# Moving the overflow branch of a mixture-of-experts layer ahead of its first gate product

## The chip, the cores and the metric

The kernel runs on one core of one Trainium2 chip. The metric is device time in microseconds (us) of one execution. A core has five engines with a queue of instructions each: PE (matrix products; its weight loads, PEld, are shown apart), DVE and ACT (vectors), POOL, and SP, which here only issues transfers (DMA) from the chip's memory. The engines wait for each other through semaphores.

## What is computed

Two layers, each a token mixer (a convolution module in the first, retention in the second) and then a mixture of experts over 256 tokens of width 1024. Each token goes to its best group of 8 experts and there to the best two. Cut to what matters:

```python
combine = jnp.sum(jax.nn.one_hot(expert_id, N_EXPERTS) * gates[..., None], axis=1)
for e in range(N_EXPERTS):                        # 32 experts, width 512
    h = jax.nn.silu(xt @ w_gate[e]) * (xt @ w_up[e])
    y = y + combine[:, e:e + 1] * (h @ w_down[e])
x = layer_norm(alpha * x + y)
```

All in float32. The weights of the experts are 6 MiB each, 192 MiB a layer, and are read once.

## The kernel before, in words

**Capacity and overflow.** Only an expert's own tokens go through its weights. The kernel gives each expert 64 places (`CAP`). `posm` holds for each token and expert the place it has, or 0; a token with place 65 or higher overflows. What overflows is worked off by `overflow`, a loop over all experts that is entered by a branch alone: `over` marks the overflowing places, a small product sums it over the tokens (`flag` in the trace, L1028), DVE adds the 64 sums up (L1031) and makes an integer of it (L1032). All five engines load that number into a register (L1203) and branch on it (L1208). With these inputs no token overflows, so every engine jumps over the body. On PE and SP the body is long (84 rows on PE as merged below, nearly 150 on SP).

**The experts.** `experts` goes through the 32 experts; each has four steps `gate_up(e, i)` of 8 matmul instructions of 512 columns (gate and up, two slices of the width each), then `hidden` (SiLU on ACT, a product on DVE, which gives `h`), `turn` (transposes of `h` on PE, `hT`), and later, two experts at a time, `down` and `scatter`. The tokens of four experts at a time are collected by one-hot products: `gather(qd, qs)`, in four quarters of the width. A quarter (`gp` in the trace) is 8 matmul instructions of 256 columns and a copy from the accumulators by ACT; the quarters 0 and 1 fill `xghi`, which the steps 0 and 1 of an expert read, the quarters 2 and 3 fill `xglo` for the steps 2 and 3.

**The weights' homes.** `Weights` loads pieces of 1 MiB in the order of use into a ring of 12 homes (`RING`), and beside it into a few others. `used(n)` gives the homes of consumed pieces back, and at once issues the next loads on SP's queue, each of which waits there until PE has read the home's old piece. So the loads run ahead of PE by the ring's size at most. When an expert stage starts, all homes are full.

**The order around the change.** It is written out by hand. In `experts`, before: two quarters of the first gather, then the rest of the routing on DVE (`rest`, which gives the gates and the marks), `gate_up(0, 0)`, the other two quarters, `turned` (transposes of `posm`, and the flag's product), `gate_up(0, 1)` to `(0, 3)`, and then `extra`, which loads the flag and branches. Its scratch (`spare`) takes two homes of the ring, so the two homes that step (0, 3) gives back are counted free only behind it (`W.used(2)`). Behind the branch come the scaling of `cur` by ACT (L1228), `hidden(0)` and the next expert. The two homes that step (0, 1) gave back are loaded ahead of the branch. Where the body is jumped over, each engine runs a short replacement that brings the semaphores to where the body would have left them; SP's part of it waits for all transfers in flight on its eight semaphores (L1208).

Of the kernel before, what the change touches and what calls it, by code (L numbers as in the profile page):

```python
# [10 lines left out]
F32 = mybir.dt.float32  # L11
# [4 lines left out]
OP = mybir.AluOpType  # L16
AX = mybir.AxisListType

P = 128
# [6 lines left out]
CAP = 64  # L26
# [5 lines left out]
RING = 12  # L32
# [17 lines left out]
class Weights:  # L50
# [4 lines left out]
    def __init__(self, nc, ringp, splitp, handp, pieces, layers):  # L55
        self.nc, self.ringp, self.splitp, self.handp = nc, ringp, splitp, handp
        self.pieces, self.layers = pieces, layers
        self.next = 0
        self.tiles, self.parts = {}, {}
        self.order = [2 * i + j for i, (_, sp) in enumerate(pieces) if sp for j in range(2)]  # L60
        self.nsplit = 0
        self.nused = 0
        self.at = 0
        self.between = []
        self.stop = len(pieces)
        self.room = {"ring": RING, "own": 0, "split": 0, "once": 0}
        self.taken = []
        self.own = None

    def home(self, i):  # L70
        for a, b in self.layers:
# [19 lines left out]
    def load(self, n=99):  # L91

        for _ in range(n):
            while self.next in self.tiles:
                self.next += 1
            for i in range(self.next, len(self.pieces)):
                home, kind = self.home(i)
                if i not in self.tiles and (self.room[home] or home != "once"):
                    break
            else:  # L100
                return
            if not self.room[home]:
                return
            self.room[home] -= 1
            src = self.pieces[i][0]
            dma = self.nc.sync.dma_start
            if home == "split" or kind:
                m = src.shape[1] // 2
                v = []
                for h, tag in enumerate(("hd", "hd") if kind == "hand" else ("hi", "lo")):  # L110
                    t = (self.handp if kind == "hand" else self.splitp).tile([P, m, 1024 // m], F32, tag=tag, name=f"w{i}{h}")
                    dma(t, src[:, h * m:(h + 1) * m])
                    v += [t[:, k] for k in range(m)]
                self.tiles[i] = v
                continue
            t = (self.own if home == "own" else self.ringp).tile([P, 2048], F32, tag=home, name=f"w{i}",
                                                                 bufs=2 if home == "own" else RING)
            if isinstance(src, list):
                v = t.rearrange("p (g a b) -> p g a b", g=2, b=P)
                for g in range(2):  # L120
                    dma(v[:, g], src[g])
                    if self.between:
                        self.between.pop(0)()
                v = [v[:, g] for g in range(2)]
            else:
                v = t.rearrange("p (a b) -> p a b", a=src.shape[1])
                dma(v, src)
                if not self.pieces[i][1]:
                    v = [v[:, k] for k in range(src.shape[1])]
            self.tiles[i] = v  # L130
# [32 lines left out]
        t, self.tiles[i] = self.tiles[i], None  # L163
        return t

    def spare(self, name):

        t = self.ringp.tile([P, 2048], F32, tag="ring", name=name, bufs=RING)
        return t[:, 0:1024], t[:, 1024:2048]

    def used(self, n=1):

# [14 lines left out]
def trunk(ctx, tc, a, out):  # L187
    nc = tc.nc
    ET = mybir.EngineType
    V, S, G, PE = nc.vector, nc.scalar, nc.gpsimd, nc.tensor  # L190
# [8 lines left out]
    def acc1(name):  # L199
        return psum.tile([P, 512], F32, tag="acc", name=name, bufs=4)  # L200
# [5 lines left out]
    def sm1(name, dt=F32):  # L206
        return psum.tile([P, 512], dt, tag="sm", name=name, bufs=4)
# [14 lines left out]
    for p in range(NE // 2 - 1):  # L222
        e, both = 2 * p + 2, (2 * p, 2 * p + 1)
# [37 lines left out]
    W = Weights(nc, ringp, splitp, handp, pieces, layers)  # L261
# [31 lines left out]
    onesb = consts.tile([P, P], BF, name="onesb")  # L293
# [134 lines left out]
    mark = {}  # L428
# [519 lines left out]
    def route(L, ep, lg, comb, posm, posT, flag):  # L948
# [3 lines left out]
        def words(n):  # L952
            used[0] += n
            return space[:, used[0] - n:used[0]]

        def t2(n):
            t = words(2 * n)
            return t.rearrange("p (a b) -> p a b", a=2) if n > 1 else t

        def t2b():  # L960

            return words(NE).bitcast(BF).rearrange("p (a b) -> p a b", a=2)

        def bc(x, n):
            return x[:, :, None].to_broadcast([P, 2, n])
# [40 lines left out]

        def rest():

            pg = t2(1)
            V.tensor_reduce(pg, gs, op=OP.add, axis=AX.X)  # L1010
            g1 = t2(1)
            V.scalar_tensor_tensor(g1, ex, 1.0, pg, op0=OP.add, op1=OP.mult)
            V.reciprocal(g1, g1)
            V.tensor_tensor(ex, ex, g1, op=OP.mult)
            V.tensor_tensor(oh1, oh1, bc(g1, 32), op=OP.mult)
            V.tensor_tensor(oh2, oh2, bc(ex, 32), op=OP.mult)
            V.tensor_tensor(comb, oh1, oh2, op=OP.add)
            posb = t2b()
            V.tensor_copy(posb, posm)
            over = t2b()  # L1020
            V.tensor_scalar(over, posm, CAP + 1.0, None, op0=OP.is_ge)

            def turned():
                pt = sm1("posT", BF)
                for tt in range(2):
                    PE.transpose(pt[:NE, tt * P:(tt + 1) * P], posb[:, tt], identb)
                fp = sm1("flag")
                PE.matmul(fp[:1, 0:64], onesb[:, 0:1], over.rearrange("p a b -> p (a b)"), start=True, stop=True)  # L1028
                V.tensor_copy(posT, pt[:NE, :T])
                ff = words(1)[:1]  # L1030
                V.tensor_reduce(ff, fp[:1, 0:64], op=OP.add, axis=AX.X)  # L1031
                V.tensor_copy(flag, ff)  # L1032

            return turned

        mark["rest"] = rest

    def experts(L, mp, ep, x1h, x1l, comb, posm, posT, flag):
# [22 lines left out]
        def gate_up(e, i):  # L1061

            if i == 0:
                gus[e] = acc1(f"gu{e}")
            if i % 2 == 0:
                gws[e] = W.take(), W.take()
            for k in range(2):
                kt = i * 2 + k
                l = xg[e // 4][kt // 4][:, kt % 4, e % 4 * CAP:(e % 4 + 1) * CAP]
                for m, w in enumerate(gws[e]):  # L1070
                    PE.matmul(gus[e][m * CAP:(m + 1) * CAP], l, w[i % 2 * 2 + k], start=kt == 0, stop=kt == KT - 1)  # L1071
            if i % 2:
                gws.pop(e)
                if (e, i) != (0, 3):
                    W.used(2)

        def hidden(e):
            gu = gus.pop(e)
# [122 lines left out]
        def extra():  # L1201

            rv = nc.values_load(flag[0:1, 0:1], min_val=0, max_val=T * NE)  # L1203
            (wts, big), mid = [W.spare(f"ov{n}{L}") for n in range(2)]
            mid = [ep.tile([P, 512], F32, tag="gl", name="ovgl")[:CAP], *[m[:CAP] for m in mid]]
            row = ep.tile([P, T], F32, tag="s0", name="ovs", bufs=2)
            pair = [acc1(f"ov{n}") for n in range(2)]
            with tc.If(rv > 0):  # L1208
                overflow(L, x1h, x1l, comb, posm, wts, big, mid, row, pair)
        fin, seeds = {}, {}  # L1210
        identr = ep.tile([P, P], F32R, name="identr")
        G.tensor_copy(identr, ident)
        W.stop = layers[L][1]
        one_hots(0)
        warm(WARM[5])
        gather(0, range(2))
        turned = mark["rest"]()
        for e in range(NE):
            for i in range(4):
                gate_up(e, i)  # L1220
                if e == 0 and i == 0:
                    gather(0, range(2, 4))
                    turned()
                if e == 0 and i == 3:
                    extra()
                    W.used(2)
                    for tt in range(2):
                        S.activation(cur[:, tt], cur[:, tt], AF.Copy, scale=ALPHA)  # L1228
                if i == 3:
                    hidden(e)  # L1230
                run(e, i)
                if e + 4 < NE and e % 4 == 1 and i == 0:
                    one_hots(e // 4 + 1)
                if e + 2 < NE and e % 4 == 2:
                    gather(e // 4 + 1, [i])
                if (e, i) in ROWS_AT:
                    n = ROWS_AT.index((e, i))
                    if n == 0:
                        rows = mp.tile([P, 2048], F32, tag="x1h", name=f"rows{L}")
                    spread_rows(L, rows, n)  # L1240
            if L == 0 and e == 3:
                mark["rot"] = rotary_tables()
            if L == 0 and e == 10:
                mark["rot"]()
# [139 lines left out]
```

## Time and profile before

| | |
|---|---|
| median of 3 runs | 1292.09 us (1291.44 to 1296.46) |
| profiled execution | 1292.11 us |
| its span in the trace | 1290.4 us |
| PE busy | 1246.8 us (97%) |
| DVE, ACT, POOL busy | 490.5, 338.7, 139.9 us |
| data moved | 459.45 MB, mean 356 GB/s |

PE's busy time counts matmuls that wait in the array's queue for their operands, so 97% does not mean that PE works at its peak. The transfers run at 425 to 427 GB/s in the middle of both expert stages. The stages of the experts last from about 138 to 597 us and from about 820 us to the end; the places that the change touches are the first 20 us of each.

### The profile page before, as it was taken

The numbers are of one execution on the slowest core, as the hardware profiler recorded it, in microseconds if no ns is written. First come the engines' busy times: TensorE is split into PE (matmuls) and PEld (weight loads), VectorE is DVE, ScalarE is ACT, GpSimd is POOL, SyncE is SP. The second block draws the span as 40 slices with busy tenths as digits, with TensorE's granted clock in tenths as the row PEclk, the third lists the DMA queues.
The fourth block names the chain that finished last, engine by engine and source line by source line (L and its number), as shares of the span: only waits on it lengthen the run. The fifth ranks groups of instructions, "written<-read, shape, count | busy, mean of one in ns | idle before, by whom it ended". The sixth has DMA issues, their size and how long they took to land.

```text
span 1290.4 us, 15546 instructions
## 1 busy us (share of the span) xinstructions
PE 1246.8 (97%) x6163; PEld 659.6 (51%) x6163; DVE 490.5 (38%) x863; ACT 338.7 (26%) x561; POOL 139.9 (11%) x167
## 2 busy tenths in 40 slices
PE   9989899999999999998999999899999999999996
PEld 7867444343443334434997788544443444444432
DVE  5986313222232222235566755413222232222224
ACT  4655311121111111123434543411111211111111
POOL 4882008100000000002130000000000000000000
PEclk9999799999999999998999999899999999999998
DMA  9935699999999999999865556699999999999993
GB/s 321 398 116 175 224 391 426 425 425 425 424 427 425 425 425 425 426 427 409 290 197 180 179 196 197 261 382 405 422 425 426 425 427 425 425 426 424 427 426 137
DMA packets 102390, 459.45 MB, mean 356 GB/s; under 512 B 8258, under 2 KB 25442, under 8 KB 59554
## 3 DMA queue, kind: packets, MB, share of 16 engines
q1 hardware_dynamic: 102082, 457.92, 88.2%
q8 instruction: 53, 0.87, 0.3%
q0 software_dynamic: 80, 0.26, 0.1%
q10 hardware_dynamic: 144, 0.15, 0.1%
q14 instruction: 31, 0.25, 0.0%
HBM read 457.25 MB, written 1.05 MB: 355 GB/s over the span
## 4 chain that ended last, share of the span: by engine, by line
PE 60%; DMA 25%; DVE 2%; ACT 1%; issue 0%; DVEq 0%; SPq 0%; ACTq 0%
PE gu L1071 22%; DMA w<-in_moe_w_up_dram 11%; DMA w<-in_moe_w_down_dram 11%; PE y L1126 10%; PE gp L1057 4%; PE sc L1158 3%; DMA w<-in_moe_w_gate_dram 2%; PE vg L788 2%; PE vg L790 2%; PE vg L789 2%; PE hT L1091 1%; PE qk L771 1%; PE qk L770 1%; PE qk L768 1%; PE wo L656 1%; PE wo L657 1%
## 5 line engine op out<-in xcount | busy, mean ns | idle before, releaser
L1071 PE MATMUL gu<-w,xghi 128*64 128x512 f32 x1024 | 250.5, 606 | 1.9 <-DMA w<-in_moe_w_up_dram 1.0
L1126 PE MATMUL y<-w,h 128*64 128x512 f32 x960 | 240.9, 596 | 7.5 <-DMA w<-in_moe_w_down_dram 7.4
L1071 PE MATMUL gu<-w,xglo 128*64 128x512 f32 x1024 | 242.6, 600 | 0.0
L1082 DVE TENSOR_TENSOR h<-gl,gu 64x512 f32<-64x512 f32 x64 | 67.7, 1058 | 368.4 <-ACT gl L1080 368.4
L1126 PEld LDWEIGHTS y<-w,h 128*64 128x64 f32 x960 | 73.4, 137 | 151.8 <-issue 134.2
L1071 PEld LDWEIGHTS gu<-w,xglo 128*64 128x64 f32 x1024 | 69.7, 137 | 117.5 <-issue 107.9
L1071 PEld LDWEIGHTS gu<-w,xghi 128*64 128x64 f32 x1024 | 67.8, 137 | 110.4 <-issue 101.2
L143 DVE TENSOR_TENSOR l<-w,h 128x1024 fp32r<-128x1024 f32 x66 | 83.6, 1269 | 68.7 <-ACT h L142 67.1
L142 ACT ACTIVATE h<-w 128x1024 fp32r<-128x1024 f32 x72 | 75.7, 1058 | 88.0 <-PE vg L790 31.7
L1080 ACT ACTIVATE gl<-gu 64x512 f32<-64x512 f32 x64 | 37.7, 589 | 229.0 <-PE gu L1071 229.0
L1104 ACT ACTIVATE h<-hT 128x256 f32<-128x256 f32 x64 | 24.7, 385 | 261.3 <-PE hT L1101 148.9
L1162 DVE TENSOR_TENSOR cur<-sc,cur 128x512 f32<-128x512 f32 x112 | 69.5, 683 | 19.0 <-PE sc L1158 19.0
L1113 DVE COPY gsl<-hT 64x1 f32<-64x1 f32 x60 | 9.4, 156 | 169.8 <-ACT h L1104 169.4
L1057 PE MATMUL gp<-oh,x1h 128*128 128x256 f32 x256 | 59.0, 313 | 3.7 <-DVE route L1010 3.7
L1057 PEld LDWEIGHTS gp<-oh,x1h 128*128 128x128 f32 x256 | 40.5, 196 | 40.5 <-issue 39.6
L1146 ACT ACTIVATE yh<-y,gsl 128x512 fp32r<-128x512 f32 x60 | 41.2, 687 | 75.8 <-PE y L1126 75.6
L466 PE MATMUL pw<-xT,w 128*128 128x256 f32 x256 | 57.8, 381 | 1.6 <-DMA w<-in_conv_w_pw_dram 1.6
L499 POOL TENSOR_TENSOR gp<-gp,gt 128x256 f32<-128x256 f32 x76 | 56.3, 742 | 22.0 <-ACT gt L498 16.6
L143 POOL TENSOR_TENSOR l<-w,h 128x1024 fp32r<-128x1024 f32 x6 | 14.9, 2516 | 364.1 <-ACT h L142 364.1
L466 PEld LDWEIGHTS pw<-xT,w 128*128 128x128 f32 x256 | 48.2, 190 | 8.9 <-issue 2.5
L1057 PE MATMUL gp<-oh,x1l 128*128 128x256 f32 x256 | 52.6, 288 | 0.0
L1139 DVE TENSOR_SCALAR s<-sp,cc 128x256 fp32r<-128x256 f32 x30 | 14.5, 484 | 86.0 <-PE sp L1136 86.0
(322 smaller groups left out, 1585.1 us busy)
## 6 DMA issues: line engine op xcount, KB each, us to landing
w<-in_moe_w_up_dram SPq DMA_DIRECT2D x116, 1024.0 KB, 15.8
w<-in_moe_w_down_dram SPq DMA_DIRECT2D x112, 1024.0 KB, 17.1
w<-in_moe_w_gate_dram SPq DMA_DIRECT2D x106, 1024.0 KB, 14.7
w<-in_ret_w_qkvg_dram SPq DMA_DIRECT2D x24, 1024.0 KB, 13.2
w<-in_moe_w_gate_dram SPq DMA_DIRECT2D x44, 512.0 KB, 14.7
w<-in_moe_w_down_dram SPq DMA_DIRECT2D x32, 512.0 KB, 17.2
w<-in_moe_w_up_dram SPq DMA_DIRECT2D x24, 512.0 KB, 17.2
w<-in_conv_w_pw_dram SPq DMA_DIRECT2D x16, 512.0 KB, 6.3
```

The costliest lines, as they stand in the source:

```text
L142: self.nc.scalar.activation(hi, w, AF.Copy)
L143: (self.nc.gpsimd if pool else self.nc.vector).tensor_tensor(lo, w, hi.bitcast(F32), op=OP.subtract)
L466: PE.matmul(ps[:, 1 - g], w[g][:, kt], xT[:, kt], start=kt == 0, stop=kt == KT - 1)
L499: G.tensor_tensor(gps[c], gps[c], t, op=OP.add)
L1057: PE.matmul(ps[:, k], src[:, tt, q * 2 + k], o[:, tt].rearrange("p e c -> p (e c)"), start=i == 0, stop=i == 3)
L1071: PE.matmul(gus[e][m * CAP:(m + 1) * CAP], l, w[i % 2 * 2 + k], start=kt == 0, stop=kt == KT - 1)
L1080: S.activation(gl, gu[:CAP], AF.Silu)
L1082: V.tensor_tensor(hs[e].rearrange("s k p -> s p k"), gl.rearrange("s (p k) -> s p k", k=4), gu[CAP:].rearrange("s (p k) -> s p k", k=4), o ...
L1126: PE.matmul(ys[pr][b][j * CAP:(j + 1) * CAP], hs[e][:, kt], wds[e][kt % 2][:, n * 512:(n + 1) * 512], start=kt == 0, stop=kt == 3)
L1146: S.activation(yh[:, n], ys[pr][n], AF.Copy, scale=g)
L1158: PE.matmul(ps, s0[pr][ks, tt * P:(tt + 1) * P], ys[pr][i][ks, n if pr >= 0 else 0], start=not held and i == 0, stop=i == 1 and (pr == -1 ...
L1162: V.tensor_tensor(o, ps, o, op=OP.add)
```

## The change

Per expert stage: the marks `over` are computed first in `rest`. `rest` is called ahead of the first gather, and gives back two functions: `flagged` (the flag's product and its two steps on DVE) and `turned` (the transposes of `posm`). Then come quarter 0, `flagged`, the quarters 1 and 2, and the branch; behind it `gate_up(0, 0)` and `(0, 1)`, quarter 3, `turned`, and `gate_up(0, 2)`, `(0, 3)`. The scratch of the body no longer takes free homes: `lend` hands out the three last loaded pieces of the ring, the body writes over them, and loads them anew from memory at its end, inside the branch.

```diff
+                if home == "ring":
+                    self.raw[i] = t, v, src
...
-    def spare(self, name):
-
-        t = self.ringp.tile([P, 2048], F32, tag="ring", name=name, bufs=RING)
-        return t[:, 0:1024], t[:, 1024:2048]
+    def lend(self, n):
+
+        held = sorted(i for i, v in self.tiles.items() if v is not None and i in self.raw)[-n:]
+        return [self.raw[i] for i in held]
...
         def rest():
 
+            over = t2b()
+            V.tensor_scalar(over, posm, CAP + 1.0, None, op0=OP.is_ge)
...
-            over = t2b()
-            V.tensor_scalar(over, posm, CAP + 1.0, None, op0=OP.is_ge)
+
+            def flagged():
+                fp = sm1("flag")
+                PE.matmul(fp[:1, 0:64], onesb[:, 0:1], over.rearrange("p a b -> p (a b)"), start=True, stop=True)
+                ff = words(1)[:1]
+                V.tensor_reduce(ff, fp[:1, 0:64], op=OP.add, axis=AX.X)
+                V.tensor_copy(flag, ff)
...
-                if (e, i) != (0, 3):
-                    W.used(2)
+                W.used(2)
...
-            (wts, big), mid = [W.spare(f"ov{n}{L}") for n in range(2)]
-            mid = [ep.tile([P, 512], F32, tag="gl", name="ovgl")[:CAP], *[m[:CAP] for m in mid]]
+            lent = W.lend(3)
+            (wts, big), mid, (sg, _) = [(t[:, 0:1024], t[:, 1024:2048]) for t, _, _ in lent]
+            mid = [sg[:CAP, 0:512], *[m[:CAP] for m in mid]]
...
                 overflow(L, x1h, x1l, comb, posm, wts, big, mid, row, pair)
+                for _, v, src in lent:
+                    nc.sync.dma_start(v, src)
...
-        gather(0, range(2))
-        turned = mark["rest"]()
+        flagged, turned = mark["rest"]()
+        gather(0, [0])
+        flagged()
+        gather(0, [1, 2])
+        extra()
         for e in range(NE):
             for i in range(4):
                 gate_up(e, i)
-                if e == 0 and i == 0:
-                    gather(0, range(2, 4))
+                if e == 0 and i == 1:
+                    gather(0, [3])
                     turned()
                 if e == 0 and i == 3:
-                    extra()
-                    W.used(2)
                     for tt in range(2):
                         S.activation(cur[:, tt], cur[:, tt], AF.Copy, scale=ALPHA)
```

PE's queue at the start of the first expert stage, before (`gp00` to `gp03` are the quarters of the gather, `gu0` is expert 0, `flag` the flag's product, `w` the weights):

```order
L1057 MATMUL gp01_1288<-oh0_1274,x1l_1109 128x256 x2
L1071 MATMUL gu0_1307<-w12_205,xghi0_1276 64x512
...
L1057 MATMUL gp02_1312<-oh0_1274,x1h_1108 128x256 x2
...
L1057 MATMUL gp03_1322<-oh0_1274,x1l_1109 128x256 x2
...
L1028 MATMUL flag_1335<-route0_1225,onesb_126 1x64
...
L1071 MATMUL gu0_1307<-w15_400,xglo0_1277 64x512
L1203 TENSOR_LOAD flag_1113
L1208 COMPARE_AND_BRANCH
...
L1071 MATMUL gu1_1740<-w16_493,xghi0_1276 64x512
```

The same place of PE's queue now:

```order
L1062 MATMUL gp00_1287<-oh0_1274,x1l_1109 128x256 x2
L1028 LDWEIGHTS onesb_126
L1028 MATMUL flag_1297<-route0_1225,onesb_126 1x64
L1062 MATMUL gp01_1301<-oh0_1274,x1h_1108 128x256 x2
...
L1062 MATMUL gp02_1311<-oh0_1274,x1l_1109 128x256 x2
L1207 TENSOR_LOAD flag_1113
L1213 COMPARE_AND_BRANCH
...
L1076 MATMUL gu0_1695<-w12_205,xghi0_1285 64x512
...
L1062 MATMUL gp03_1708<-oh0_1274,x1h_1108 128x256 x2
```

The branch has moved from behind the 32 matmul instructions of expert 0 to ahead of them; between the flag's product and the load of the flag stand two quarters of the gather now, where three steps of expert 0 stood.

SP's queue around the branch of the first expert stage, before (`w31` to `w34` are the first pieces that are loaded into homes that expert 0 gave back):

```order
L127 DMA w31_1344<-in_moe_w_up_dram 128x2048
L127 DMA w32_1346<-in_moe_w_gate_dram 128x2048
L1203 TENSOR_LOAD flag_1113
L1203 ISA x2
L1208 COMPARE_AND_BRANCH
...
L1208 UNCONDITIONAL_BRANCH
L127 DMA w33_1730<-in_moe_w_up_dram 128x2048
L127 DMA w34_1732<-in_moe_w_gate_dram 128x2048
```

SP's queue there now:

```order
L113 DMA w291_1223<-in_moe_w_down_dram 128x1024
L1207 TENSOR_LOAD flag_1113
L1207 ISA x2
L1213 COMPARE_AND_BRANCH
...
L1216 DMA w24_1054<-in_moe_w_down_dram 128x2048
L1213 UNCONDITIONAL_BRANCH x2
L128 DMA w31_1704<-in_moe_w_up_dram 128x2048
L128 DMA w32_1706<-in_moe_w_gate_dram 128x2048
```

The loads of `w31` and `w32` have moved behind the branch; ahead of it stand only the loads that fill the homes for the first time. The three loads of L1216 are the refill, inside the body.

ACT's queue there now (`xglo` from `gp03` is the copy of quarter 3, which stood ahead of the flag's load before):

```order
L1064 ACTIVATE xglo0_1286<-gp02_1311 128x512
L1207 TENSOR_LOAD flag_1113
L1213 COMPARE_AND_BRANCH
...
L1064 ACT_TABLE_LOAD
L1064 ACTIVATE xglo0_1286<-gp03_1708 128x512
L1236 ACTIVATE cur_75<-cur_75 128x1024 x2
L1084 ACT_TABLE_LOAD
L1084 ACTIVATE gl0_1736<-gu0_1695 64x512
```

The copy of quarter 3 has moved behind the branch; the scaling of `cur`, the second table load and the SiLU of expert 0 follow it as before.

## Rows read from the trace of the kernel before

**Rows 1.** The page: the chain that ended last, by engine.

```profile
PE 60%; DMA 25%; DVE 2%; ACT 1%; issue 0%; DVEq 0%; SPq 0%; ACTq 0%
```

**Rows 2.** Timeline, first expert stage: start, us, engine, line, operation, tiles, count, [idle before <-releaser].

```profile
137.96 0.77 PE L1057 MATMUL gp<-oh,x1h 128*128 128x256 f32 x2 [1.86 <-DVE route L1010]
140.10 0.60 ACT L1059 ACTIVATE xghi<-gp 128x512 f32<-128x512 f32 x1 [2.92 <-PE gp L1057]
141.64 2.66 PE L1071 MATMUL gu<-w,xghi 128*64 128x512 f32 x8
146.43 0.19 PE L1028 MATMUL flag<-route,onesb 128*1 128x64 bf16 x1
147.08 0.14 DVE L1032 CAST flag<-route 1x1 int32<-1x1 f32 x1
148.32 3.60 PE L1071 MATMUL gu<-w,xglo 128*64 128x512 f32 x16
150.14 2.00 ACT L1228 ACTIVATE cur<-cur 128x1024 f32<-128x1024 f32 x2
152.11 1.94 PE L1071 MATMUL gu<-w,xghi 128*64 128x512 f32 x8 [0.19 <-PEq L1208]
152.16 1.28 ACT L1080 ACT_TABLE_LOAD   x1
154.07 1.03 DVE L1082 TENSOR_TENSOR h<-gl,gu 64x512 f32<-64x512 f32 x1 [6.85 <-ACT gl L1080]
155.25 0.43 PE L1091 MATMUL hT<-ident,h 64*128 64x64 f32 x4 [1.20 <-DVE h L1082]
```

**Rows 3.** Timeline, second expert stage, same columns.

```profile
820.68 0.76 PE L1057 MATMUL gp<-oh,x1h 128*128 128x256 f32 x2 [1.85 <-DVE route L1010]
829.76 0.14 DVE L1032 CAST flag<-route 1x1 int32<-1x1 f32 x1
835.26 1.94 PE L1071 MATMUL gu<-w,xghi 128*64 128x512 f32 x8 [0.66 <-PEq L1208]
837.83 0.43 PE L1091 MATMUL hT<-ident,h 64*128 64x64 f32 x4 [0.63 <-DVE h L1082]
```

**Rows 4.** Windows, the first stage's stretches behind its start: DMA share and GB/s last.

```profile
155.00:158.00 3.00, 2.75 (x14) 1.43 (x16) 1.11 (x4) 0.39 (x1) 0.00 (x0) 0.80 0.14 49
158.00:160.00 2.00, 2.00 (x8) 0.61 (x6) 0.00 (x0) 0.00 (x0) 0.00 (x0) 0.50 0.60 115
176.00:178.00 2.00, 2.00 (x11) 0.58 (x8) 1.05 (x1) 0.59 (x1) 0.00 (x0) 1.00 0.92 270
192.00:194.00 2.00, 2.00 (x10) 1.16 (x7) 1.26 (x2) 0.00 (x0) 0.00 (x0) 1.00 0.85 252
198.00:300.00 102.00, 102.00 (x508) 41.82 (x506) 24.72 (x41) 18.57 (x34) 31.61 (x40) 1.00 1.01 426
```

**Rows 5.** Windows, the second stage's stretches behind its start, same columns.

```profile
837.00:841.00 4.00, 3.37 (x22) 1.69 (x22) 1.68 (x4) 0.38 (x1) 0.00 (x0) 1.00 0.25 100
884.00:887.00 3.00, 3.00 (x16) 1.01 (x14) 0.77 (x1) 0.00 (x0) 0.00 (x0) 1.00 1.00 350
```

**Rows 6.** Waits of SP's queue, 155 to 200 us: total us, times, longest.

```profile
SPq L127 <- PE gu L1071: 25.4, 6, 6.9
```

**Rows 7.** Lines L1203 and L1208: ns min/median/max, first and last start in us.

```profile
L1203 PEldq TENSOR_LOAD <-flag x2: 317/402/488, 147.8 to 830.7; - x2
L1208 ACTq COMPARE_BRANCH  x2: 45/45/45, 148.0 to 830.5; - x2
L1208 PEldq COMPARE_BRANCH  x2: 3362/3670/3979, 148.4 to 831.1; - x2
```

**Rows 8.** DMA queues, 148.4 to 151.8 us: packets, MB, share of the engines.

```profile
q8 instruction: 1, 0.02, 1.9%
```

**Rows 9.** Windows with PE's granted clock third from the end (0.50 is 1.2 GHz).

```profile
156.79:160.20 3.41, 3.41 (x12) 0.97 (x8) 0.89 (x3) 0.00 (x0) 0.00 (x0) 0.50 0.42 91
836.04:839.45 3.41, 2.78 (x18) 1.36 (x16) 1.23 (x3) 0.95 (x2) 0.00 (x0) 1.00 0.58 238
```

More of the change, by code (lines that the diff above doesn't have):

```diff
@@ L68, in __init__ @@
         self.own = None
+        self.raw = {}
     def home(self, i):
@@ L1026, in turned @@
                     PE.transpose(pt[:NE, tt * P:(tt + 1) * P], posb[:, tt], identb)
-                fp = sm1("flag")
-                PE.matmul(fp[:1, 0:64], onesb[:, 0:1], over.rearrange("p a b -> p (a b)"), start=True, stop=True)
                 V.tensor_copy(posT, pt[:NE, :T])
[L1030 to L1034, printed above, removed]
+            return flagged, turned
         mark["rest"] = rest
```

## The prediction, made before the changed kernel was run

> **What bounds the kernel now.** I read the page first, then the timeline at the start of both expert stages, then the windows of the transfers, then the lines of the branch. The chain on the page is 60% PE and 25% DMA [rows 1]: PE sets the time in long stretches, and in others PE waits for weights. Which of the two holds where is seen in the windows: from 198 us on the transfers of the first expert stage run at 426 GB/s without a break [rows 4], so the end of that stage is set by when that unbroken stream began and by its length. The question for a change in the first 20 us is therefore whether it moves the start of the unbroken stream, or only something ahead of it.
>
> Behind the branch of before SP is stopped until all transfers have landed, and the windows show it: 49 GB/s from 155 to 158 us and 115 from 158 to 160 [rows 4], 100 GB/s from 837 to 841 us in the second stage [rows 5]. Against 426 GB/s that is 3 x (1 - 49/426) + 2 x (1 - 115/426) = 4.1 us of transfer time in the first stage and 4 x (1 - 100/426) = 3.1 us in the second. But it does not stand at the end of anything: later the rate falls again, to 270 GB/s at 176 us and 252 at 192 us [rows 4], to 350 at 884 us [rows 5], and between 155 and 200 us SP's queue waits six times for PE's gate products, 25.4 us in all and 6.9 at the longest [rows 6]. There the loads had caught up: every home was full, and SP waited for PE to give one back. From then on the start of the stream is set by PE's pace, not by the stop. What counts is when PE gets through expert 0, and I measure it at the first transposes of `hT`, the first work that needs the whole of expert 0: 155.25 us [rows 2] and 837.83 us [rows 3]. A shift there shifts the releases at 176 to 197 us, so the stream, so the end.
>
> **The change part by part, first stage.** A quarter of the gather takes (141.64 - 137.96) / 2 = 1.84 us there [rows 2], at the low clock level. So quarter 0 ends at 139.8, and with the flag's product (0.1) and two more quarters PE is through at 143.5. The mark `over` is moved within DVE's work ahead of the product, and costs PE nothing since the first product waits for the one-hots ahead of it.
>
> From the start of the flag's product to the integer are 147.08 + 0.14 - 146.43 = 0.79 us [rows 2], so the flag stands at 140.7. From there to PE's branch were 148.4 - 147.22 = 1.18 us, with the register load at 147.8 [rows 2, 7]. PE's queue does this while products still wait in front: at 147.8 the 16 products that start at 148.32 had not begun [rows 2, 7]. So the branch starts at 141.9, beside quarters 1 and 2.
>
> Then comes the dear part. PE's compare-and-branch took 3362 ns and 3979 ns, ACT's 45 ns [rows 7], and while PE's ran, one packet of 16 KB (0.02 MB) came on an instruction queue [rows 8]. So PE's jump over the long body costs a fetch. Before, that lay beside 16 products of 3.60 us [rows 2], and only 0.19 us [rows 2] and 0.66 us [rows 3] of idle time showed. Now its cover is what is left of the two quarters, 143.5 - 141.9 = 1.6 us. Bounds for the branch: 0.05 us (ACT's row) and 3.98; I take 3.36, the row that it is nearest to, as the data transfers are silent at this time. Before, the next product came 152.11 - (148.40 + 3.36) = 0.35 us behind it. So the first gate product starts at 141.9 + 3.36 + 0.35 = 145.6, after 2.1 us of idle PE.
>
> The Trainium skill, "Runtime: NRT & Kernel Launch", section Instruction fetch mechanics, says that a taken branch to a page that is not already held must wait for a transfer of that page; the packet and the 3.4 us agree with it. The Trainium skill, "Advanced Engine Details and Errata", section Control Flow Timing, gives a compare-and-branch about 108 ns; PE's row is more than thirty times that, so the measurement decides, and what the small figure would make of the sum is the third rival.
>
> From there, both steps (0, 0) and (0, 1) are 16 products, 3.6 us, and quarter 3 at the high clock 0.92: done at F + 4.5, with F the first product. Then ACT decides: the copy of the quarter 0.60, the two scalings of `cur` 2.00, the table load 1.28, and from its end (153.44) to `hT` 155.25 - 153.44 = 1.81 [rows 2]; in sum F + 10.2. PE's own work to there (16 products 3.6, the step (1, 0) 1.94 [rows 2]) ends at F + 10.1, so the gap of 1.20 us ahead of `hT` [rows 2] nearly closes. `hT` comes at 155.8, 0.5 us late.
>
> To this comes the clock. Rows 9 show that after the 1.2 us gap (with only small transposes behind it) PE was granted 1.2 GHz for 3.41 us, in which it does half the work: 1.7 us lost. After the gaps of 0.66 and 0.63 us in the second stage it kept the 2.4 GHz [rows 3, 9]. The new gap of 2.1 us may bring such a stretch, the old one at 156.8 should go. For the new one the bounds are 0 and 1.7 us; one row speaks for each, and I take the middle, 0.85. First stage: 0.5 + 0.85 - 1.7 = -0.35 us.
>
> **Second stage.** Quarter 0 ends at 820.68 + 1.84 = 822.5, all three at 826.3. The flag stands at 823.4, the branch starts 831.1 - 829.90 = 1.2 us later [rows 3, 7], at 824.6, and ends at 828.0; the first product starts at 828.2 (0.18 behind it, 835.26 - 835.08 [rows 3, 7]), after 1.9 us of idle PE. `hT` comes at 838.4, 0.5 us late; there is no old stretch to lose, so 0.5 + 0.85 = +1.35 us.
>
> **The loads.** The loads of `w31` and `w32` wait for step (0, 1), which ends at F + 3.6 = 149.2 instead of 148.3; those of `w33` and `w34` come right after step (0, 3) and not after the stop. SP's stop now falls ahead of them, when everything has landed. That is a gain in transfer time of some 4 and 3 us, as above, and I cost it at nothing since the loads wait for PE at 176 us anyhow; they will only wait longer there. The refill is inside the body and is not run. POOL has nothing that PE waits for there.
>
> **The sum** is made against the profiled execution, 1292.11 us (span 1290.4), 0.02 us over the median of the three runs: 1292.1 - 0.35 + 1.35 = 1293.1.
>
> **The rivals.** First, the stop is worth what it lost: the stream of either stage begins earlier by the 4.1 and 3.1 us, since the starved end of the stage covers what PE loses at its start. Then 1292.1 - 7.2 = 1284.9. For it speaks that DMA ends 25% of the chain [rows 1]; against it the falls to 270, 252 and 350 GB/s with SP waiting for PE [rows 4 to 6]. If only a part of the lost time had been made good, the truth lies between. Chance 0.14.
>
> Second, on the other side: PE's branch is not hidden at all. If PE's queue loads the flag only when the quarters in front have run, the load and the compare (0.6) and the longer fetch (3.98) follow on 143.5 and 826.3, the first products come at 148.4 and 831.1, 2.9 us later than forecast in both stages, and the half clock follows surely (0.85 more each): 1293.1 + 5.8 + 1.7 = 1300.6. It decides from the point where the register load starts later than about 143 us. For it: PE has less in front of the branch than ever before. Against it: the load at 147.8 ahead of 16 waiting products [rows 7]. Chance 0.11.
>
> Third, the branch is cheap there (0.05 to 0.1 us, the fetch done ahead): no gap, so 2.0 and 1.8 us less and no new stretch at half clock (0.85 each): 1293.1 - 3.8 - 1.7 = 1287.6. Against it both rows of PE [rows 7]. Chance 0.06.
>
> **How the numbers follow.** My forecast, PE's pace decides and the branch is half covered, has 0.69; by the bounds of the branch and the clock it lies between 1288 and 1298. A measurement of this kernel can't tell less than 0.5% (6.5 us) from no change. The range reaches to the first and nearly to the second rival, 1285 to 1300. Faster by over 0.5% (under 1285.6): more than half of the first rival and a little of the third, 0.11. Slower (over 1298.6): most of the second and a tail of the forecast, 0.11. The rest, 0.78, is within.
>
> **What will show it.** In the timeline: the flag's integer near 140.7 and 823.4 us, PE's compare-and-branch of over 3 us beside the quarters 1 and 2, an idle PE of about 2 us ahead of the first gate product, and `hT` within 1 us of 155.25 and 837.83 (2 us with a stretch at half clock). In the windows: no stop of the transfers at 155 to 160 us, and a deeper fall at 176 us. I am wrong if the transfers run unbroken from about 150 us on and the end comes 4 us earlier per stage, or if PE idles for 4 us ahead of the first gate product.

## The result: half a per cent slower, beyond what was forecast

The changed kernel takes 1301.94 us (median of 6 runs, 1298.11 to 1304.52), the kernel before 1295.66 us beside it (6 runs, 1291.44 to 1297.09). The ratio of the runs is 1.0058, with a 95% interval of 1.0039 to 1.0077: 5.0 to 10.0 us slower. The forecast was 1293.1 us, no change, and the range ended at 1300.

The profiled execution took 1300.68 us (span 1298.9). Its timeline at the start of the first expert stage, the rows that answer to [rows 2] (L1062 is the gather, L1076 `gate_up`, L1084 `gl`, L1095 `hT`, L1213 the branch, L1236 the scaling of `cur`):

```profile
141.28 0.76 PE L1062 MATMUL gp<-oh,x1h 128*128 128x256 f32 x2 [1.56 <-DVE route L1013]
143.75 0.14 DVE L1031 CAST flag<-route 1x1 int32<-1x1 f32 x1
146.08 0.40 PE L1062 MATMUL gp<-oh,x1l 128*128 128x256 f32 x2
147.81 1.28 ACT L1064 ACT_TABLE_LOAD   x1 [0.70 <-ACTq L1213]
148.97 5.30 PE L1076 MATMUL gu<-w,xghi 128*64 128x512 f32 x16 [2.50 <-PEq L1213]
155.56 3.65 PE L1076 MATMUL gu<-w,xglo 128*64 128x512 f32 x16
155.95 1.99 ACT L1236 ACTIVATE cur<-cur 128x1024 f32<-128x1024 f32 x2
159.04 1.89 PE L1076 MATMUL gu<-w,xghi 128*64 128x512 f32 x8
159.33 1.28 ACT L1084 ACT_TABLE_LOAD   x1 [1.39 <-PE gu L1076]
160.63 0.59 ACT L1084 ACTIVATE gl<-gu 64x512 f32<-64x512 f32 x1
161.25 1.03 DVE L1086 TENSOR_TENSOR h<-gl,gu 64x512 f32<-64x512 f32 x1 [5.30 <-ACT gl L1084]
162.33 0.46 PE L1095 MATMUL hT<-ident,h 64*128 64x64 f32 x4 [1.40 <-DVE h L1086]
```

PE stands twice: 2.50 us ahead of the first gate product, released by the branch, and 1.40 us ahead of `hT`, where [rows 2] had 1.20. Between the last product of step (0, 3) and `hT` lies one chain: table load, `gl`, `h`. The table load waits for PE, not for the scalings ahead of it. The second stage, answering to [rows 3]:

```profile
826.20 0.76 PE L1062 MATMUL gp<-oh,x1h 128*128 128x256 f32 x2 [1.86 <-DVE route L1013]
828.67 0.14 DVE L1031 CAST flag<-route 1x1 int32<-1x1 f32 x1
833.72 3.65 PE L1076 MATMUL gu<-w,xghi 128*64 128x512 f32 x16 [1.80 <-PEq L1213]
838.66 3.65 PE L1076 MATMUL gu<-w,xglo 128*64 128x512 f32 x16
839.04 1.99 ACT L1236 ACTIVATE cur<-cur 128x1024 f32<-128x1024 f32 x2
842.43 1.28 ACT L1084 ACT_TABLE_LOAD   x1 [1.39 <-PE gu L1076]
845.43 0.46 PE L1095 MATMUL hT<-ident,h 64*128 64x64 f32 x4 [1.40 <-DVE h L1086]
```

ACT has scaled `cur` at 839.04 + 1.99 = 841.03 us; the table load starts 1.39 us later, when PE is through step (0, 3) at 838.66 + 3.65 = 842.31.

From the gather's start to `hT` are 162.33 - 141.28 = 21.05 and 845.43 - 826.20 = 19.23 us; before they were 17.29 and 17.15 [rows 2, 3]. That is 3.76 and 2.08 us more.

The branch, line L1213 (ns min/median/max, first and last start), answering to [rows 7]:

```profile
L1213 PEldq COMPARE_BRANCH  x2: 3867/3868/3870, 144.8 to 829.5; - x2
L1213 ACTq COMPARE_BRANCH  x2: 45/45/45, 147.3 to 832.7; - x2
```

The windows (the last two columns are DMA share and GB/s, the third from the end PE's granted clock), answering to [rows 4] and, the row at 148.90, to [rows 9]:

```profile
148.90:152.30 3.40, 3.33 (x8) 1.11 (x10) 0.00 (x0) 0.20 (x1) 0.00 (x0) 0.50 0.02 5
158.00:160.00 2.00, 2.00 (x12) 0.67 (x10) 0.00 (x0) 0.67 (x1) 0.00 (x0) 1.00 1.01 426
180.00:184.00 4.00, 4.00 (x22) 1.60 (x19) 1.05 (x1) 0.98 (x2) 0.00 (x0) 1.00 0.51 150
198.00:300.00 102.00, 102.00 (x508) 42.89 (x508) 25.64 (x43) 17.22 (x32) 33.89 (x43) 1.00 1.01 422
```

The stop at 158 us is gone, and the loads wait for PE later and longer: 150 GB/s at 180 us, and SP's queue, answering to [rows 6], waits 35.2 us for gate products where it waited 25.4. The line is of 155 to 205 us; 158.3 to 203.3 us, the stretch of [rows 6] shifted by the 3.3 us that this stage begins later, gives 35.2 as well.

```profile
SPq L128 <- PE gu L1076: 35.2, 7, 6.9
```

From the gather's start to the last `gl` of the stage the two stages took 452.55 + 451.89 us, and 450.62 + 448.94 before: 4.9 us of the difference of the two spans (8.5) lie there. 3.3 of the rest arise ahead of the first gather, where one execution had a stretch at half clock at 9.0 us that the other had not. They are the spread of single executions: in the 14 traces of this case the first gather starts between 137.76 and 142.22 us, at 140.2 on average with the new order and with the old.

### The profile page after: what moved, and what is told of

Same layout as the page of the kernel before. It is cut to its first block, busy times and chain, and to the rows that moved or that the text cites. A ratio compares the mean times of both kernels' runs of the same rounds, so it can differ in the third digit from the quotient of the medians.

```text
span 1298.9 us, 15551 instructions
## 1 busy us (share of the span) xinstructions
PE 1249.2 (96%) x6163; PEld 664.0 (51%) x6163; DVE 490.9 (38%) x863; ACT 338.5 (26%) x561; POOL 139.6 (11%) x167
## 5 line engine op out<-in xcount | busy, mean ns | idle before, releaser
L1076 PE MATMUL gu<-w,xghi 128*64 128x512 f32 x1024 | 249.1, 604 | 5.4 <-PEq L1213 4.3
L1076 PE MATMUL gu<-w,xglo 128*64 128x512 f32 x1024 | 242.7, 599 | 0.0
L1076 PEld LDWEIGHTS gu<-w,xglo 128*64 128x64 f32 x1024 | 69.3, 136 | 115.6 <-issue 106.4
L1076 PEld LDWEIGHTS gu<-w,xghi 128*64 128x64 f32 x1024 | 68.3, 137 | 113.7 <-issue 102.3
L1084 ACT ACTIVATE gl<-gu 64x512 f32<-64x512 f32 x64 | 37.7, 589 | 229.2 <-PE gu L1076 229.1
L1108 ACT ACTIVATE h<-hT 128x256 f32<-128x256 f32 x64 | 24.6, 385 | 260.0 <-PE hT L1105 147.6
L1062 PE MATMUL gp<-oh,x1h 128*128 128x256 f32 x256 | 59.9, 317 | 3.4 <-DVE route L1013 3.4
L1062 PEld LDWEIGHTS gp<-oh,x1h 128*128 128x128 f32 x256 | 41.1, 199 | 40.3 <-issue 39.3
L1062 PE MATMUL gp<-oh,x1l 128*128 128x256 f32 x256 | 52.9, 289 | 0.0
L1162 PE MATMUL sc<-yh,s 128*128 128x512 f32 x112 | 47.1, 420 | 0.0
```

Source lines behind the costliest of these rows:

```text
L1062: PE.matmul(ps[:, k], src[:, tt, q * 2 + k], o[:, tt].rearrange("p e c -> p (e c)"), start=i == 0, stop=i == 3)
L1084: S.activation(gl, gu[:CAP], AF.Silu)
L1162: PE.matmul(ps, s0[pr][ks, tt * P:(tt + 1) * P], ys[pr][i][ks, n if pr >= 0 else 0], start=not held and i == 0, stop=i == 1 and (pr == -1 ...
```

## The experiments

The theory: PE's jump over the long body now shows as idle time, and what PE loses goes straight to `hT` and to the end of the stage. The rivals: the new order of gather, routing and loads costs; the homes cost; nothing in the stages costs, and the difference arises ahead of them. Every ratio is to the kernel before, run beside it on the same chip, with its 95% interval. Each diff shows the lines that matter; those of `late_nobranch` and `lent_late` are made in the kernel before, the others in the changed kernel unless something else is said.

**No branch, new order** (`early_nobranch`) and **no branch, old order** (`late_nobranch`).

```diff
         gather(0, [1, 2])
-        extra()
```

> The changed kernel without its branch and without the body: the flag is still computed and nobody reads it, tokens that overflow would not be worked off. Theory (PE's uncovered jump is the cost): the idle 2.50 and 1.80 us ahead of the first gate product go, and the stretch at half clock behind the first of them with them (up to 1.7 us), so 4.3 to 6.0 us less than the changed kernel: 1296 to 1297.6, with the first gate product 7.7 - 2.3 = 5.4 us behind the gather's start in both stages. Rival (the new order costs: the routing's rest ahead of the gather, quarter 3 behind two steps, the loads of w31 and w32 later): 1300 to 1302, as the changed kernel. Rival (the difference between the two kernels arises ahead of the gather, 3.3 us in the profiled pair): 1298 to 1300.

1296.9 us, 1.0016 (1.0002 to 1.0030). The first gate product follows the gather without a wait, 5.5 and 5.8 us behind its start, and `hT` comes at 17.25 and 17.79 us. Without the branch most of the loss is gone, which bears out the theory and speaks against the first and third rival as the main cause. Some 2 us (0.3 to 3.9) are left over the kernel before; the last run below is about them.

```diff
-                if (e, i) != (0, 3):
-                    W.used(2)
+                W.used(2)
...
                 if e == 0 and i == 3:
-                    extra()
-                    W.used(2)
```

> The kernel before without its branch, body and spare homes (overflow would not be worked off): step (0, 3) gives its two homes back at once, and SP is never stopped. Theory (the stop is worth nothing, and the jump lies beside products): 1294 to 1296, less than 2 us under the kernel before; the loads run from 155 us without a stop and wait longer for PE at 176 us. Rival (the stop is worth the transfer time that it lost, 4.1 and 3.1 us): 1288.5.

1295.45 us, 1.0004 (0.9990 to 1.0018): where it stood, the branch cost nothing that can be measured, nor did SP's stop. The windows show the trade that the prediction had named: no stop, and a deeper fall behind it (213 GB/s where [rows 4] have 270, 203 for 252; the stage begins 1.7 us later here). From 155 to 200 us SP's queue waits 30.2 us for gate products, where it waited 25.4 [rows 6].

```profile
158.00:160.00 2.00, 2.00 (x13) 0.84 (x14) 1.01 (x3) 0.39 (x1) 0.00 (x0) 1.00 1.04 438
176.00:178.00 2.00, 2.00 (x12) 0.49 (x8) 0.79 (x1) 0.59 (x1) 0.00 (x0) 1.00 0.88 213
192.00:194.00 2.00, 2.00 (x11) 1.01 (x8) 1.26 (x2) 0.00 (x0) 0.00 (x0) 1.00 0.95 203
```

**The homes alone** (`lent_late`): the branch behind expert 0 as before, its scratch lent and loaded anew.

```diff
-            (wts, big), mid = [W.spare(f"ov{n}{L}") for n in range(2)]
+            lent = W.lend(3)
...
-                if (e, i) != (0, 3):
-                    W.used(2)
+                W.used(2)
```

> The home part of the change alone: the scratch is in three lent pieces which the body loads anew, step (0, 3) gives its homes back at once, and the branch stays behind expert 0, where it was. Theory (homes and load order cost and give nothing, the branch's place is all): 1295 to 1296.5, as the kernel before. Rival (the lent homes cost, by a longer body or by loads that now stand ahead of SP's stop): 1298 to 1302.

1294.03 us, 1.0005 (0.9990 to 1.0020). The homes cost and give nothing that can be measured; what the changed kernel lost came with the branch's place and the order around it. SP's stop is still there, only later: no transfer from 164 to 166 us.

**More products in front of the jump**: one step (`cover8`) and two (`cover16`).

```diff
-        gather(0, [1, 2])
-        extra()
+        gather(0, [1, 2])
...
                 gate_up(e, i)
+                if e == 0 and i == 0:      # cover16: i == 1, ahead of gather(0, [3])
+                    extra()
```

> The changed kernel with the branch one step later, behind gate_up(0, 0): 8 products of 512 columns (1.8 us) more stand between the flag and PE's jump. Theory (uncovered jump): the idle time at the branch falls from 2.50 and 1.80 us to 0.7 and 0.1, so 3.5 us less than the changed kernel and up to 1.7 less for the half clock: 1296.7 to 1298.5. Rival (the order costs, not the jump): 1300 to 1302. Rival (PE does not run ahead of the products, so cover does not help): 1301 to 1302 with the idle time as it was.

> The changed kernel with the branch two steps later, behind gate_up(0, 1) and ahead of quarter 3: 16 products (3.6 us) more in front of PE's jump. With 8 more the branch began 1.0 to 1.2 us later behind the flag, so only a part of the 1.8 us counted as cover. Theory (uncovered jump): the idle PE at the branch falls from 2.50 and 1.80 us to 0.2 to 0.7 (it was 0.19 and 0.66 in the kernel before with the same 16 products in front), hT comes 17.3 to 18.0 us behind the gather's start, and the time is 1296 to 1298. Rival (cover is given back, since PE's queue comes to the branch only so far ahead of the products): idle 1.3 us as with 8 products and 1300 to 1301.

cover8: 1300.56 us, 1.0047 (1.0029 to 1.0066), idle at the branch 1.36 and 0.58 us. cover16: 1299.0 us, 1.0032 (1.0015 to 1.0049), idle 1.45 and 0.91 us. Both missed what the theory forecast, and cover16 came to the rival's idle time, if not to its total. The total of cover8 cannot be told from the changed kernel's (1.0058, 1.0039 to 1.0077). The timeline of cover16's PE in the first stage:

```profile
147.30 3.81 PE L1076 MATMUL gu<-w,xghi 128*64 128x512 f32 x16
152.56 0.47 PE L1062 MATMUL gp<-oh,x1h 128*128 128x256 f32 x2 [1.45 <-PEq L1213]
```

and its register load and branches:

```profile
L1207 PEldq TENSOR_LOAD <-flag x2: 320/404/487, 147.6 to 831.3; - x2
...
L1213 ACTq COMPARE_BRANCH  x2: 45/45/45, 148.2 to 831.6; - x2
L1213 PEldq COMPARE_BRANCH  x2: 3274/3646/4019, 148.2 to 831.8; - x2
```

The flag's integer stood at 144.1 us there, but PE's queue came to its load at 147.6, 3.6 us later, when 14 products had not begun. In all traces with the long body these products are 12 to 18 at the load and 10 to 14 at the branch, never more, however many were written in front (up to 32 in cover16). So the cover is bounded: some 12 products of 512 columns, at 3.60 / 16 = 0.225 us each, are 2.7 us against a jump of 3.3 to 4.0. The kernel before had 14 such products left at its branch, in both stages, and that is why only 0.19 and 0.66 us [rows 2, 3] showed.

**A body without the loop** (`refill_body`): flag, load and branch stay, PE's body is nearly empty.

```diff
             with tc.If(rv > 0):
-                overflow(L, x1h, x1l, comb, posm, wts, big, mid, row, pair)
                 for _, v, src in lent:
```

> The changed kernel with a body that only reloads the three pieces: the loop over the experts is left out (tokens that overflow would not be worked off), the flag's load and the branch stay on all engines, and on PE the jump passes over next to nothing. Theory (the dear part is the fetch of code that lies far away): PE's compare-and-branch takes under 1 us, PE does not wait ahead of the first gate product, and the time is that without a branch, 1296 to 1298. Rival (any taken branch of PE costs a fetch, whatever its length): 3.4 to 3.9 us as before, idle 2.5 and 1.8 us, 1301 to 1302.

1297.93 us, 1.0019 (1.0003 to 1.0034), and the branch takes PE a seventeenth of the time:

```profile
L1207 PEldq TENSOR_LOAD <-flag x2: 312/400/488, 144.1 to 827.9; - x2
...
L1213 PEldq COMPARE_BRANCH  x2: 211/224/236, 144.9 to 828.3; - x2
```

PE does not idle ahead of the first gate product. What is jumped over is what costs: 1.0058 less 1.0019 is 0.39%, 5.0 us (1.9 to 8.2 by the two intervals), against 2.50 + 1.80 us of idle time and, in the profiled execution, a stretch at half clock (3.40 us behind the first of them, 1.7 lost). The Trainium skill, "Runtime: NRT & Kernel Launch", section Instruction fetch mechanics, has a taken branch wait for a fetch when its target lies outside the pages held. The rows agree with it in part: 3.87 us over the long body and 0.22 us over next to none are as it has them, but the half body below gave either time for the same code.

The run also takes away ACT's table load behind the branch (1.28 us at 147.81 in the changed kernel); there ACT had nothing to do until 155.45 us, so that load held up nothing.

**The table load taken out of the chain ahead of `hT`** (`after_silu`; `preload` is a SiLU on one column).

```diff
         extra()
+        preload(AF.Silu)
```

> The changed kernel with a one-column SiLU on ACT right behind the branch, so that SiLU's table is loaded there, in place of the load that ACT makes behind every branch anyway (147.81 us), and not between the last product of step (0, 3) and gl. Theory (PE's lateness goes straight through the unchanged chain last product, table load 1.28, gl, h, hT): 1.3 us less ahead of hT in each stage, so hT at 19.7 and 17.9 us behind the gather's start, and 2.6 us less than the changed kernel, up to 3.4 less when the stretches at half clock behind that gap go too: 1298 to 1299.5. Rival (the gap ahead of hT is covered by something else that is late, the weights or PE's queue): hT earlier, but the time as it was, 1301 to 1302.

1297.83 us, 1.0025 (1.0010 to 1.0040): 0.33%, 4.3 us less than the changed kernel (1.2 to 7.4 by the two intervals), where 2.6 to 3.4 were forecast. In its timeline ACT loads one table behind the branch, and `gl` follows the last product at once:

```profile
146.79 1.28 ACT L364 ACT_TABLE_LOAD   x1 [0.70 <-SPq L1213]
147.51 5.35 PE L1076 MATMUL gu<-w,xghi 128*64 128x512 f32 x16 [2.05 <-PEq L1213]
157.92 0.59 ACT L1084 ACTIVATE gl<-gu 64x512 f32<-64x512 f32 x1 [1.41 <-PE gu L1076]
159.65 0.46 PE L1095 MATMUL hT<-ident,h 64*128 64x64 f32 x4
```

**The same with the branch behind expert 0** (`late_silu`: lent_late with that line behind `extra()`).

```diff
                     extra()
+                    preload(AF.Silu)
```

> lent_late (the branch behind expert 0, its scratch in lent pieces) with the same one-column SiLU right behind the branch, ahead of the scalings of cur: ACT loads one table there and not two. Theory (ACT's chain sets hT in the kernel before): hT 1.0 to 1.3 us earlier in both stages (PE's step (1, 0) covers the rest), and no stretch at half clock behind that gap (1.7 us in one stage of the two in each trace so far): 1291.5 to 1293.5. Rival (the end of a stage is set by the transfers alone, and a gap at its start is worth nothing): 1294 to 1296.

1292.77 us, 0.9985 (0.9970 to 0.9999): below both kernels, by 0.15% of the one before. `hT` comes at 15.78 and 16.91 us with no gap ahead of it.

**Half the body** (`after_rolled`, `after_rolled_silu`, `late_rolled_silu`): three copies of the inner loop rolled into one, 118 instead of 236 instructions on PE (products counted without their weight loads).

```diff
-            for r in range(1, T // CAP):
+            with tc.For_i(1, T // CAP):
+                nc.vector.tensor_scalar(pe, pe, -float(CAP), None, op0=OP.add)
...
```

> The changed kernel with the body's inner loop over the three further blocks of places rolled up (a loop in place of three copies; the places are counted down by 64 in each pass): PE's body shrinks from 236 to 118 instructions, and does the same. Theory A (the cost goes by whether the target lies in code that the queue has already fetched, and half the length is near enough): compare-and-branch of PE under 0.5 us, no idle time ahead of the first gate product, 1297 to 1298 as with the body that only reloads. Theory B (half the length is still too far): 3.4 to 3.9 us, idle 2.5 and 1.8 us, 1301 to 1302. Theory C (the fetch grows with the length): about half, 1.7 to 2 us, idle up to 0.5 us, 1298 to 1299.

> The same rolled body, and the one-column SiLU behind the branch, which gave 4 us in the changed kernel. Theory A: both gains add, hT at 16 to 16.5 us behind the gather's start in both stages, 1292 to 1294. Theory B: as the changed kernel with SiLU, 1297 to 1298. Theory C: 1294 to 1295.5.

> The branch behind expert 0 with lent homes and the one-column SiLU, with the rolled body. Its idle time at the branch is 0.2 and 0.8 us. Theory A: these go, and the time is up to 1 us less than with the long body, 1291.5 to 1293. Theory B: as with the long body, 1292.5 to 1293.5.

after_rolled: 1301.04 us, 1.0067 (1.0049 to 1.0086), its six runs from 1296.28 to 1307.24. after_rolled_silu: 1295.21 us, 1.0017 (1.0004 to 1.0030). late_rolled_silu: 1292.12 us, 0.9992 (0.9981 to 1.0003). PE's branch in the three, in this order:

```profile
L1213 PEldq COMPARE_BRANCH  x2: 450/1900/3350, 143.2 to 827.2; - x2
```
```profile
L1213 PEldq COMPARE_BRANCH  x2: 2507/3198/3890, 141.4 to 823.8; - x2
```
```profile
L1211 PEldq COMPARE_BRANCH  x2: 318/335/352, 150.4 to 830.9; - x2
```

None of the three theories holds: at half the length the same jump is cheap (0.32 to 0.45 us) in three cases and dear (2.5 to 3.9) in three. Where it is cheap PE waits 0.30 us (first stage of after_rolled) or 0.19 us (both stages of late_rolled_silu), and 0.19 us is also what it waited in the kernel before, behind a jump of 3.36 us: that much is not the jump. At the early place rolling saved nothing that can be measured. after_rolled and after_rolled_silu differ by the one-column SiLU on ACT alone, and yet the jump of the first stage took 0.45 us in one and 2.51 us in the other; so the length of the body does not decide by itself.

**What the order alone costs** (`early_nobranch_silu`).

```diff
         gather(0, [1, 2])
-        extra()
+        preload(AF.Silu)
```

> The changed kernel without its branch and body (tokens that overflow would not be worked off), with the one-column SiLU where the branch stood. It asks what the new order itself costs when neither the jump nor the table load stands in it: without a branch it was 0.16% (2 us) over the kernel before. Theory (the order costs nothing, those 2 us lie in the gap of 1.4 us ahead of hT and the stretches at half clock behind it): hT at 16 us behind the gather's start in both stages, no stretch at half clock behind it, 0.1 to 0.25% under the kernel before, as late_silu. Rival (rest ahead of the gather, quarter 3 late and the first loads late cost 2 us by themselves): hT at 16 us too, but the time as the kernel before or up to 0.1% over it.

1291.75 us, 0.9979 (0.9963 to 0.9996), as the theory had it; `hT` came at 15.12 and 15.58 us. With the preload the new order costs nothing that can be measured. That the 2 us of `early_nobranch` lay in its gaps ahead of `hT`, as the theory had it, is not shown: they are 1.39 us in both stages, but so are those of `late_nobranch`, which equals the kernel before, and each of the two has one stretch at half clock behind them. The intervals of the two overlap (1.0002 to 1.0030, 0.9990 to 1.0018), so the 2 us may be nothing.

Over the 14 traces: behind a gap of 0.6 to 1.4 us ahead of `hT` PE fell to half clock for 3.4 us in 8 of 18 stages, behind none or 0.15 us in 0 of 10. One of the eight, in `refill_body` (granted clock third from the end):

```profile
161.00:164.40 3.40, 3.40 (x10) 0.97 (x8) 0.36 (x1) 0.00 (x0) 0.00 (x0) 0.51 0.83 280
```

## Why the prediction failed, point by point

**The start of the first gate product was right, in part by luck.** Foreseen at 7.6 and 7.5 us behind the gather's start (145.6 - 137.96, 828.2 - 820.68), it came at 7.69 and 7.52, with 2.50 and 1.80 us of idle PE (2.1 and 1.9 foreseen). Two errors cancelled: the branch began 3.5 and 3.3 us behind the gather's start where 3.9 was foreseen in both, and took 3.87 us where 3.36 was. The second rival, PE's jump not hidden at all, gave a total near the measured one (1300.6), but by another way: it wanted the first product 2.9 us later.

**The step that failed is "the gap of 1.20 us ahead of `hT` nearly closes".** It put `hT` 10.2 us behind the first gate product, as the sum of ACT's copy, scalings, table load and 1.81. Measured are 845.43 - 833.72 = 11.71 us in the second stage and 13.36 in the first, 1.65 of them by the half clock. The sum let ACT run from its copy without a break; but the table load stands in front of a SiLU that needs PE's last product of step (0, 3), and ACT waited 1.39 us for it. The prediction's own figures had this wait: by them ACT is through the scalings at F + 4.5 + 0.60 + 2.00 = F + 7.1, and PE through step (0, 3) at F + 4.5 + 3.6 = F + 8.1. The trace of the kernel before had it too, in the second stage, where a gap of 0.63 us stood ahead of `hT` [rows 3]:

```profile
834.72 1.28 ACT L1080 ACT_TABLE_LOAD   x1 [0.42 <-PE gu L1071]
```

What is behind the last product (table load 1.28, `gl`, `h`) takes as long as ever, so PE's lateness passes through it undiminished. With 11.7 in place of 10.2 the shift of `hT` is 2.0 us per stage instead of 0.5, and the sum 1293.1 + 2 x 1.5 = 1296.1, against 1292.1 before; these 4.0 us are still under the measured 5.0 to 10.0. `after_silu` bears the step out: with the table load out of the chain, 4.3 us are given back. And a late `hT` does reach the end: over the 14 traces, one execution each, the two stages together (gather's start to the last `gl`) are 1.1 us longer for each us that the two `hT` come later (correlation 0.90, scatter 1.3 us).

**The clock was mis-sized in one point.** The old stretch at 156.8 us was counted as a loss that goes (-1.7). It was a matter of the single execution: the kernel before had it in one stage of two, like 8 of 18 stages with such a gap, and the changed kernel kept the gap. The new stretch, costed at 0.85 per stage, came in the first (1.65) and not in the second. Without the 1.7 the sum put right is 1297.8, 5.7 us over 1292.1 and within the measured 5.0 to 10.0; this is an estimate, with the same odds of the old stretch in both kernels, and the profiled execution of the changed kernel happened to have none there.

**The base was low.** The sum stood on 1292.1 us, the median of three runs of the kernel before; the median of six is 1295.66. So 3.6 of the 8.8 us between the forecast of 1293.1 and the measured 1301.94 belong to no step of the prediction, and on its own base a loss of 0.58% would have come to 1299.6, inside its range. A loss beyond the noise it would have been all the same: the six runs told 0.58% to within 0.19, where the prediction had held 0.5% to be the least that can be told.

**The loads were right.** The stop's removal is worth nothing that can be measured: `late_nobranch`, which has no stop, is at most 0.10% (1.3 us) under the kernel before by its interval, where the first rival wanted 7.2 us. That refutes it. The third, a cheap branch, is what `refill_body` makes of it; with the long body it did not happen.

**What stays open.** 4.9 us are located in the stages of the profiled pair; the ratio says 5.0 to 10.0. Whether the middle of that interval holds 2 us more that belong to the change, no run tells. Nor do they tell what decides between a cheap and a dear jump over the rolled body. The packet of [rows 8] is no proof that the branch waits for it: in `refill_body`, too, an instruction packet (0.01 MB) moved beside a branch of 0.24 us.

## What to carry to other kernels

Each jump over the long body cost PE 3.3 to 4.2 us, and only work already queued right in front covered it; ask how many instructions that queue really holds ahead, and put the branch where these are the longest ones. Where a chain is summed along one engine, check each link for what it waits for on the others: the table load here stood in front of its first user and had that user's wait (1.39 us). A preload of one column cost 0.20 us and its table load (1.28 us), and took the load out of the chain. And a sum stands on its base: three runs of the kernel before lay 3.6 us under the median of six.

## What the runs showed of the hardware that was not expected

- PE's queue came to a register load at most 18 products ahead of the array, whatever stood in front; 8 products more moved the branch 1.0 to 1.2 us later (behind the gather's start 3.5 and 3.3 us in the changed kernel, 4.5 and 4.6 in `cover8`).
- PE's compare-and-branch took 3.27 to 4.15 us over the long body (236 instructions in the changed kernel), 0.32 to 3.89 over 118 and 0.21 to 0.24 over next to none. ACT's took 0.045 in all of them. SP's took 0.05 over its long body, too, but SP's next instruction began 2.9 and 2.5 us behind it in the changed kernel and 0.1 us behind it in `refill_body`.
- Behind the branch over a body with SiLU in it ACT loads a table anew, even ahead of a plain copy (1.28 us at 147.81); in `refill_body`, which has the branch but no work of ACT in its body, the copy of quarter 3 has no load ahead of it, so the branch alone does not bring one. A SiLU placed there made that load the only one. The Trainium skill, "ScalarE activation tables: per-element evaluation and per-set limits", section Table sets in the compiler and the runtime, says that the table loads are placed block by block. The row at 147.81 agrees, since a branch begins a block; `refill_body` shows that a new block need not begin with a load.
- A gap of 0.6 to 1.4 us in front of a few small transposes was followed by 3.4 us at half clock in 8 of 18 cases: there it cost itself and some 1.7 us more.
